# Norms of two key blocks as four rows: one root and one reciprocal for a pair, spread to the lanes by small products

## The chip, the cores and the metric

The kernel runs on one core of a Trainium2 chip. The metric is the time of one execution on the device, in microseconds (us), the median of several runs. TensorE (PE in the profile, its weight loads PEld) multiplies and writes to PSUM, VectorE (DVE) and ScalarE (ACT) work on SBUF and PSUM, GpSimd (POOL) on SBUF, SyncE (SP) issues most transfers. Each engine takes its instructions strictly in the order in which they stand in its queue.

## The reference, cut to what matters

The kernel computes two layers of a diffusion backbone on 128 context and 2048 latent positions (2176 in all) with 1024 channels. The change concerns the second layer, RWKV-7 time mixing, and there the keys:

```
xr, xw, xk, xv, xa, xg = [u + dx * rw['mu'][i] for i in range(N_LERP)]
k = xk @ rw['w_rkvz'][1]
kk = heads(kf * rw['k_k'].astype(f32))                       # 16 heads of 64 channels
kk = kk * lax.rsqrt(jnp.sum(kk * kk, axis=-1, keepdims=True) + 1e-12)
```

So each head's 64 channels of `kk`, at each position, are divided by the length of that vector of 64.

## The kernel before, in words

The projections of layer 1 (`phase_l1_proj`) hold channels on the partitions (lanes) and positions on the free axis. Three passes follow each other: pass 0 makes r and the decay's hidden layer, pass 1 (`wi == 1`) makes k, its normalised form kk and the hidden layer of a, the third makes v. Passes 0 and 1 go over five segments of positions (450, three times 448, and 384 columns). In each segment DVE and ACT blend the inputs (`lerp`, lines 818 and 819, after the sums of line 803), GpSimd subtracts the rounded part (line 34), and PE makes eight blocks of 128 channels (two heads each) with 24 matmuls a block (lines 832 to 835) and one more block for the hidden layer (`pl`).

For each of the eight k blocks DVE copies the product from PSUM to a tile `o` (line 867), ACT squares it into `sq` (line 871), and `normalise` follows one block later: PE multiplies `sq` with `bones`, a 128x128 matrix of two blocks of ones, so that every lane holds its head's sum (line 846, full fp32, in the trace as two matmul records); ACT takes the root (847), DVE the reciprocal (848), and one DVE operation multiplies `o`, the weight and the reciprocal (849). SP writes the result to `kkC` (line 840).

Rings of buffers tie these steps: four `sq`, five `o`, four PSUM banks for `p`, one PSUM bank for `pnt`. A new `sq` waits for the write of the block four earlier, a new `o` for the last reader of the tile five earlier.

The order on each engine is set by a scheduler when the program is built, from its own cost estimates. It is fixed in the program and shown below where it matters.

Of the kernel before, what the change touches and what calls it, by code (L numbers as in the profile page):

```python
# [7 lines left out]
F32 = mybir.dt.float32  # L8
F32R = mybir.dt.float32r
AF = mybir.ActivationFunctionType  # L10
ALU = mybir.AluOpType
# [4 lines left out]
P = 128  # L16
# [618 lines left out]
def ucol(t):  # L635
    return 1 if t == 0 else 3 + t * P
# [89 lines left out]
def phase_l1_proj(tc, g, ins):  # L726

    nc = tc.nc
# [8 lines left out]
    with ExitStack() as es:  # L737
# [33 lines left out]
        pl = es.enter_context(tc.tile_pool(name="ppl", bufs=2, space=PSUM, reuse_waits="tile"))  # L771
        pn = es.enter_context(tc.tile_pool(name="ppn", bufs=1, space=PSUM, reuse_waits="tile"))
        mu1, muh, kkw, bones, eps = g.l1

        def pieces(c0, n):

            if c0 == 1:
                return [(0, 0, LP), (LP + 2, LP, n - LP - 2)]
            return [(0, c0 - 3, n)]

        def wsplit(parts, src, ncols, ring):
            wh, wl = parts
            for c in range(0, ncols, P):
                w = next(ring)
                nc.sync.dma_start(out=w, in_=src[:, c:c + P].rearrange("(k p) c -> p k c", p=P))
                split_hi(nc, wh[:, :, c:c + P], w)
                split_lo(nc, wl[:, :, c:c + P], w, wh[:, :, c:c + P])
            return wh, wl
# [49 lines left out]
        def chunked(dst, b, o, pcs):  # L838
            for (o0, t0, ln) in pcs:
                nc.sync.dma_start(out=dst[t0 // 64:(t0 + ln) // 64, :, b, :].rearrange("c p t -> p c t"),  # L840
                                  in_=o[:, o0:o0 + ln].rearrange("p (c t) -> p c t", t=64))

        def normalise(b, o, sq, n, pcs):

            pnt = pn.tile([P, 512], F32, name="pnt")
            nc.tensor.matmul(pnt[:, :n], bones, sq[:, :n], start=True, stop=True)
            nc.scalar.activation(sq[:, :n], pnt[:, :n], AF.Sqrt, bias=eps)
            nc.vector.reciprocal(sq[:, :n], sq[:, :n])
            nc.vector.scalar_tensor_tensor(sq[:, :n], o[:, :n], kkw[:, b:b + 1], sq[:, :n], op0=ALU.mult, op1=ALU.mult)
            chunked(g.kkC, b, sq, pcs)  # L850


        for wi, (mi, si, sw, dst) in enumerate(((0, 1, "w1", g.rC), (2, 4, "a1", g.kC))):
            W = [wsplit((W0, W1)[hh], ins["w_rkvz"][wi][:, hh * 512:(hh + 1) * 512], 512, early if (wi, hh) == (0, 0) else w_ring)
                 for hh in range(2)]
            Sw = wsplit(Ws, ins[sw], P, w_ring)
            for (c0, n) in FSEG:
                pcs = pieces(c0, n)
                us = load_u(c0, n)
                ss = sums(us, n)  # L860
                xh, xl = lerp(us, ss, mi, n, 0)
                yh, yl = lerp(us, ss, si, n, 1)
                pend = []
                for b in range(KC):
                    p = fm_block(*W[b // 4], b % 4, xh, xl, n, pd, "p")
                    o = op.tile([P, 512], F32, name="o")
                    nc.vector.tensor_copy(o[:, :n], p[:, :n])
                    chunked(dst, b, o, pcs)
                    if wi == 1:
                        sq = op.tile([P, 512], F32, name="sq", bufs=4)  # L870
                        nc.scalar.activation(sq[:, :n], p[:, :n], AF.Square, scale=kkw[:, b:b + 1])
                        pend.append((b, o, sq))
                    if b == KC - 1:
                        p = fm_block(*Sw, 0, yh, yl, n, pl, "pl")
                        o = op.tile([P, 512], F32, name="o")
                        nc.scalar.activation(o[:, :n], p[:, :n], AF.Tanh if wi == 0 else AF.Copy)
                        for (o0, t0, ln) in pcs:
                            for e in range(2):
                                nc.sync.dma_start(out=g.hwa[e, 64 * wi:64 * wi + 64, t0:t0 + ln], in_=o[64 * e:64 * e + 64, o0:o0 + ln])
                    if len(pend) > 1:  # L880
                        normalise(*pend.pop(0), n, pcs)
                if pend:
                    normalise(*pend.pop(), n, pcs)

        W = [wsplit((W0, W1)[hh], ins["w_rkvz"][2][:, hh * 512:(hh + 1) * 512], 512, w_ring) for hh in range(2)]
        Sw = wsplit(Ws, ins["g1"], P, w_ring)
        for seg in TSEG:
            c0 = ucol(seg[0])
            n = ucol(seg[-1]) + P - c0
# [4 lines left out]
            p = fm_block(*Sw, 0, yh, yl, n, pl, "pl")  # L894
            o = op.tile([P, 512], F32, name="o")
            nc.scalar.activation(o[:, :n], p[:, :n], AF.Sigmoid)
            nc.scalar.dma_start(out=g.sgd[:, c0:c0 + n], in_=o[:, :n])
            for hh in range(2):
                for t in seg:
                    o0 = ucol(t) - c0  # L900
                    p = pd.tile([P, 512], F32, name="p")
# [3 lines left out]
                    o = op.tile([P, 512], F32, name="o")  # L905
# [828 lines left out]
def constants():  # L1734
    import numpy as np

    f32 = np.float32
    d = {"ident": np.eye(P, dtype=f32)}
    n = np.arange(512)
    s = 1.0 / math.sqrt(LS * 128)  # L1740
    ang = lambda k, m: 2 * np.pi * (np.outer(m, k) % LS) / LS
    d["dft"] = (np.stack([np.cos(ang(2 * n, n)), np.cos(ang(2 * n + 1, n)), np.sin(ang(2 * n, n)),
                          np.sin(ang(2 * n + 1, n + 1))]) * s).astype(f32)
    sign = np.where(np.arange(513) % 2 == 0, s, -s)
    row = np.zeros((1, 514))
    row[0, :513] = sign
    d["dft_row"] = row.astype(f32)
    col = np.zeros((P, 2))
    col[:, 0] = sign[:P]
    d["dft_col"] = col.astype(f32)  # L1750
    a = 2 * np.pi * (np.outer(np.arange(P), np.arange(P)) % P) / P
    d["c128"] = np.stack([np.cos(a), np.sin(a), np.cos(a) / P, -np.sin(a) / P], 1).astype(f32)
    m = np.full((9, P, 512), 1e30, f32)
    q = np.arange(P)
    for t, (ra, cb) in enumerate(TYPES):
        (r0, nr), (c0, ncol) = RT[ra], CT[cb]
        r, c = ra * 8 + q // 16, cb * 16 + q % 16
        kr = ra * 8 - 4 + r0 + np.arange(nr)
        kc = cb * 16 - 8 + c0 + np.arange(ncol)
        rs, cs = np.clip(r - 4, 0, 24), np.clip(c - 8, 0, 48)  # L1760
        okr = (kr[None] >= rs[:, None]) & (kr[None] < rs[:, None] + 8)
        okc = (kc[None] >= cs[:, None]) & (kc[None] < cs[:, None] + 16)
        m[t, :, :nr * ncol] = np.where(okr[:, :, None] & okc[:, None, :], 0, 1e30).reshape(P, -1)
    d["namask"] = m
    st, t, up = np.arange(P)[:, None] % 64, np.arange(64)[None], np.arange(P)[:, None] >= 64
    d["tri"] = np.stack([st < t, st <= t, np.where(up, st >= t, st <= 63 - t), np.where(up, st <= 63 - t, st >= t),
                         63 - st < t], 1).astype(f32)
    d["bones"] = np.kron(np.eye(2), np.ones((64, 64))).astype(f32)
    return d


# [61 lines left out]
```

## Time and profile before

| | |
|---|---|
| median of 3 runs | 4006.51 us (3995.91 to 4013.2) |
| the profiled execution | 4006.46 us, span 4004.7 us |
| mean granted TensorE clock | 0.905 of full speed |
| busy share of the span: PE, DVE, ACT, POOL | 88%, 65%, 43%, 20% |
| pass 1 (k), by the first of its matmuls and the first of pass v | 1641 to 1923 us of the span |

Busy shares over the whole span mix stages with different limits; pass 1 is read on its own below. A matmul's duration in the trace holds its way through the array; back-to-back matmuls overlap, so that what one costs is the distance between starts.

### The profile page before, as it was taken

The page shows a single profiled execution, that of the slowest core. Times are in us where ns is not written, and L with a number is a line of the kernel's source. Part 1 is how long each engine was busy: PE and PEld are TensorE (multiplying, and loading weights), DVE is VectorE, ACT ScalarE, POOL GpSimd, SP SyncE. Part 2 cuts the span into 40 slices and gives each one's busy share as a digit, 9 for nine tenths or more (in the row PEclk, how much of TensorE's full clock was granted, in tenths as well). Part 3 has the DMA queues.
Part 4 walks back from the last instruction along what each step waited for, and adds up shares of the span by engine and source line. Part 5 has one row for each costly group of instructions (what it writes and reads, how often), then busy time and mean ns, then how long its engine had stood idle before and what let it go on. Part 6 is the DMA issues. An engine that isn't in the chain of part 4 may idle for free. (4 is left out here: it accounts for less than half of the span.)

```text
span 4004.7 us, 93003 instructions
## 1 busy us (share of the span) xinstructions
PE 3509.4 (88%) x39520; PEld 3039.7 (76%) x39520; DVE 2597.0 (65%) x4364; ACT 1730.1 (43%) x3629; POOL 782.3 (20%) x434
## 2 busy tenths in 40 slices
PE   6999998889999979999899997888888888885677
PEld 3999997567777769888687776877888778884555
DVE  6201101478867765899862347877878878875997
ACT  5110011266645533544442344555565555543444
POOL 3000000332202223323332320000000000001665
PEclk8999998999999989999899997788778888787888
DMA  6122214565546742434315542333233233224543
GB/s 213 64 71 86 69 58 139 159 172 143 135 121 191 186 111 81 135 103 115 119 67 153 157 122 79 88 92 86 78 92 86 78 92 98 76 76 152 202 165 115
DMA packets 514383, 463.07 MB, mean 116 GB/s; under 512 B 217111, under 2 KB 420391, under 8 KB 512430
## 3 DMA queue, kind: packets, MB, share of 16 engines
q1 hardware_dynamic: 506350, 444.95, 38.1%
q10 hardware_dynamic: 7616, 12.16, 0.9%
q8 instruction: 310, 5.08, 0.5%
q14 instruction: 107, 0.88, 0.1%
HBM read 314.13 MB, written 129.48 MB: 111 GB/s over the span
## 5 line engine op out<-in xcount | busy, mean ns | idle before, releaser
L34 POOL TENSOR_TENSOR xl<-xt,xh 128x1792 fp32r<-128x1792 f32 (+4 forms) x64 | 246.8, 3867 | 487.8 <-ACT xh L30 244.3
L40 PE MATMUL p<-ul,wh 128*128 128x436 f32 (+1 forms) x800 | 291.7, 365 | 2.4 <-DVE ul L34 2.1
L38 PE MATMUL p<-uh,wh 128*128 128x436 f32 (+1 forms) x800 | 291.5, 365 | 0.0
L39 PE MATMUL p<-uh,wl 128*128 128x436 f32 (+1 forms) x800 | 289.7, 362 | 0.0
L819 DVE SCALAR_TENSOR_TENSOR xt<-s,l1s,xt 128x448 f32<-128x448 f32 (+4 forms) x256 | 246.8, 1016 | 46.7 <-ACT xt L818 46.7
L834 PE MATMUL p<-xh,w 128*128 128x448 f32 (+2 forms) x640 | 240.4, 376 | 17.7 <-ACT w L30 10.2
L1213 POOL COPY WC<-W 128x8 f32<-128x8 f32 x68 | 29.8, 438 | 1133.4 <-DVE Sc L1455 671.4
L835 PE MATMUL p<-xh,w 128*128 128x448 f32 (+2 forms) x640 | 239.7, 374 | 0.0
L30 ACT ACTIVATE xh<-xt 128x1792 fp32r<-128x1792 f32 (+4 forms) x64 | 99.8, 1570 | 226.7 <-DVE xt L819 107.0
L1265 PE MATMUL pq<-Xb,BKb 64*128 64x64 f32 x2176 | 162.5, 304 | 37.6 <-DVE OM L1276 28.2
L1340 DVE TENSOR_TENSOR xe<-xe,l1s 128x31 f32<-128x31 f32 (+15 forms) x527 | 180.8, 343 | 18.1
L1339 DVE TENSOR_TENSOR l1s<-xe,xe 128x31 f32<-128x31 f32 (+15 forms) x527 | 179.6, 341 | 16.4
L1265 PEld LDWEIGHTS pq<-Xb,BKb 64*128 64x128 f32 x2176 | 151.2, 215 | 46.8 <-DVE OM L1276 31.0
L818 ACT ACTIVATE xt<-u,l1s 128x448 f32<-128x448 f32 (+4 forms) x256 | 142.0, 625 | 61.5 <-POOL xl L34 46.0
L40 PEld LDWEIGHTS p<-ul,wh 128*128 128x128 f32 x800 | 151.8, 190 | 12.6 <-DVE ul L34 4.5
L38 PEld LDWEIGHTS p<-uh,wh 128*128 128x128 f32 x800 | 151.9, 190 | 7.8 <-ACT uh L30 0.3
L39 PEld LDWEIGHTS p<-uh,wl 128*128 128x128 f32 x800 | 152.1, 190 | 7.5
L34 DVE TENSOR_TENSOR wl<-w,wh 128x2048 fp32r<-128x2048 f32 x12 | 27.5, 2291 | 189.5 <-ACT wh L30 189.5
L832 PE MATMUL p<-xl,w 128*128 128x448 f32 (+2 forms) x640 | 148.4, 369 | 1.1 <-POOL xl L34 1.1
L434 POOL TENSOR_TENSOR kl<-ld,kh 128x1088 fp32r<-128x1088 f32 x16 | 42.2, 2659 | 547.8 <-ACT kh L433 547.5
L834 PEld LDWEIGHTS p<-xh,w 128*128 128x128 f32 x640 | 123.6, 193 | 32.5 <-ACT w L30 11.1
L1303 PE MATMUL pq<-ident,BKb 64*128 64x64 f32 x1088 | 62.0, 256 | 92.0 <-DVE OM L1276 44.8
(375 smaller groups left out, 10036.9 us busy)
## 6 DMA issues: line engine op xcount, KB each, us to landing
x<-x SPq DMA_DIRECT2D x34, 512.0 KB
zu<-u1T SPq DMA_DIRECT2D x34, 512.0 KB
kk<-kkC SPq DMA_DIRECT2D x68, 256.0 KB
k<-kC SPq DMA_DIRECT2D x68, 256.0 KB
r<-rC SPq DMA_DIRECT2D x68, 256.0 KB
sv<-v SPq DMA_DIRECT2D x136, 128.0 KB
x<-in_x_sample SPq DMA_DIRECT2D x32, 512.0 KB
wmod<-in_ada_w SPq DMA_DIRECT2D x16, 1024.0 KB
```

The costliest lines, as they stand in the source:

```text
L34: (eng or nc.vector).tensor_tensor(lo, x, hi.bitcast(F32), op=ALU.subtract)
L38: nc.tensor.matmul(out, ah, bh, start=start, stop=False)
L39: nc.tensor.matmul(out, al, bh, start=False, stop=False)
L40: nc.tensor.matmul(out, ah, bl, start=False, stop=stop)
L818: nc.scalar.activation(x[:, j], us[hh][:, j, 1:n + 1], AF.Copy, scale=mu1[:, i, k:k + 1])
L819: nc.vector.scalar_tensor_tensor(x[:, j], ss[hh][:, j, :n], muh[:, i, k:k + 1], x[:, j], op0=ALU.mult, op1=ALU.add)
L832: nc.tensor.matmul(p[:, :n], w(wh, k), xl[:, k, :n], start=False, stop=(k == KC - 1))
L834: nc.tensor.matmul(p[:, :n], w(wh, k), xh[:, k, :n], start=(k == 0), stop=False)
L835: nc.tensor.matmul(p[:, :n], w(wl, k), xh[:, k, :n], start=False, stop=False)
L1265: nc.tensor.matmul(o[:, h, p], BK[HF[h], p, 64 * h:64 * h + 128], X[HF[h], p, 0:64], start=True, stop=True)
L1339: nc.vector.tensor_tensor(t, L[:, m:, j:m].to_broadcast([P, n, m]), Tm[:, j:m, :m].to_broadcast([P, n, m]), op=ALU.mult)
L1340: nc.vector.tensor_tensor(o, o, t, op=ALU.subtract)
```

## The change

The matrix `bones` is replaced by columns: for block i of a pair, four columns that pick the two heads of that block into rows 2i and 2i+1. `normalise` now takes two blocks at a time, once three are pending. Two products (line 848 of the changed kernel) accumulate the four head sums in lanes 0 to 3; ACT takes the root and DVE the reciprocal on these four rows. For each block, second first, two products with four rows and 64 columns of a repeated column of the identity (line 856) write each head's reciprocal to its 64 lanes in PSUM, and the DVE multiplication (858) reads it there. Lines of the changed kernel stand 1 to 9 higher from here on: 867 is 876, 871 is 880, 819 is 820, 832 to 835 are 833 to 836, 847 is 850, 848 is 851.

```diff
+        heads = bones[:, 0:8].rearrange("p (i h) -> p i h", i=2)
...
-        def normalise(b, o, sq, n, pcs):
+        def normalise(pend, n, pcs):

             pnt = pn.tile([P, 512], F32, name="pnt")
-            nc.tensor.matmul(pnt[:, :n], bones, sq[:, :n], start=True, stop=True)
-            nc.scalar.activation(sq[:, :n], pnt[:, :n], AF.Sqrt, bias=eps)
-            nc.vector.reciprocal(sq[:, :n], sq[:, :n])
-            nc.vector.scalar_tensor_tensor(sq[:, :n], o[:, :n], kkw[:, b:b + 1], sq[:, :n], op0=ALU.mult, op1=ALU.mult)
-            chunked(g.kkC, b, sq, pcs)
+            for i, (b, o, sq) in enumerate(pend):
+                nc.tensor.matmul(pnt[0:4, :n], heads[:, i], sq[:, :n], start=(i == 0), stop=(i == 1))
+            inv = pend[0][2][0:4]
+            nc.scalar.activation(inv[:, :n], pnt[0:4, :n], AF.Sqrt, bias=eps[0:4])
+            nc.vector.reciprocal(inv[:, :n], inv[:, :n])
+            for i in (1, 0):
+                b, o, sq = pend[i]
+                pnt = pn.tile([P, 512], F32, name="pnt")
+                for h in range(2):
+                    nc.tensor.matmul(pnt[64 * h:64 * h + 64, :n], g.ident[0:4, 2 * i + h:2 * i + h + 1].to_broadcast([4, 64]), inv[:, :n],
+                                     start=True, stop=True)
+                nc.vector.scalar_tensor_tensor(sq[:, :n], o[:, :n], kkw[:, b:b + 1], pnt[:, :n], op0=ALU.mult, op1=ALU.mult)
+                chunked(g.kkC, b, sq, pcs)
...
-                    if len(pend) > 1:
-                        normalise(*pend.pop(0), n, pcs)
+                    if len(pend) > 2:
+                        normalise([pend.pop(0), pend.pop(0)], n, pcs)
                 if pend:
-                    normalise(*pend.pop(), n, pcs)
+                    normalise(pend, n, pcs)
...
-    d["bones"] = np.kron(np.eye(2), np.ones((64, 64))).astype(f32)
+    pair = np.kron(np.eye(2), np.ones((64, 1)))
+    d["bones"] = np.concatenate([pair, 0 * pair, 0 * pair, pair, np.zeros((P, P - 8))], 1).astype(f32)
```

On PE, inside a block of a 448 column segment, before (`xh`, `xl` are the rounded input and its rest, `w` a weight half, `pnt` the norm's bank, `l1s` the tile that holds `bones`; a row of L846 is one product):

```order
L835 MATMUL p<-xh_12258,w_12226 128x448
L834 MATMUL p<-xh_12258,w_12225 128x448
L846 MATMUL pnt<-sq,l1s 128x448 [waits Activation_49]
L835 MATMUL p<-xh_12258,w_12226 128x448
L834 MATMUL p<-xh_12258,w_12225 128x448
L835 MATMUL p<-xh_12258,w_12226 128x448
L832 MATMUL p<-xl_12259,w_12225 128x448 x8
```

On PE in a 448 column segment of the changed kernel, at the end of a block:

```order
L835 MATMUL p<-xh_12258,w_12220 128x448
L856 MATMUL pnt<-sq,ident 64x448 [waits DVE_49]
L856 MATMUL pnt<-sq,ident 64x448
L836 MATMUL p<-xh_12258,w_12221 128x448
L833 MATMUL p<-xl_12259,w_12220 128x448 x8
L856 MATMUL pnt<-sq,ident 64x448 [waits DVE_49]
L856 MATMUL pnt<-sq,ident 64x448
L848 MATMUL pnt<-sq,l1s 4x448 [waits DVE_49]
L848 MATMUL pnt<-sq,l1s 4x448
L835 MATMUL p<-xh_12258,w_12220 128x448 [waits Activation_49]
```

Where one product per block stood among the matmuls, waiting for ACT's square alone, a pair now has three places on PE, each waiting for DVE: twice for the spreading products, once for the sums, which here stand right behind the spreading products of the pair before, and use the same bank. Over the whole pass the sums follow the last spreading products of the pair before with no matmul between in 9 of 19 places; the two spreading groups of a pair stand side by side in 2 of 20; and 28 to 52 matmuls stand between the sums and the first spreading.

On DVE at the start of the pass, before (`sq` the squares, later the result; `o` the copied product):

```order
L848 RECIPROCAL sq<-sq 128x450 [waits Activation_49]
L867 COPY o<-p 128x450 [waits DMAHW2_49,DMAHW1_49,PE_49]
L849 SCALAR_TENSOR_TENSOR sq<-o,l1s,sq 128x450 [waits DVE_49]
L848 RECIPROCAL sq<-sq 128x450 [waits Activation_49]
L867 COPY o<-p 128x450 [waits DMAHW6_49,DMAHW5_49,PE_49]
L849 SCALAR_TENSOR_TENSOR sq<-o,l1s,sq 128x450 [waits DVE_49]
```

On DVE in the changed kernel, a little later in the pass:

```order
L851 RECIPROCAL sq<-sq 4x450 [waits Activation_49]
L858 SCALAR_TENSOR_TENSOR sq<-o,l1s,pnt 128x450 [waits DMAHW6_49,DMAHW5_49,PE_49]
L876 COPY o<-p 128x448 [waits DMAHW3_49,DVE_49]
L858 SCALAR_TENSOR_TENSOR sq<-o,l1s,pnt 128x450 [waits PE_49]
L876 COPY o<-p 128x448 [waits DVE_49]
L851 RECIPROCAL sq<-sq 4x448 [waits DMAHW5_49,DMAHW4_49,Activation_49]
```

One reciprocal serves two blocks; each multiplication now waits for PE, and the copies behind it wait for a multiplication, whose `o` they take over.

## Rows read from the trace of the kernel before

**Rows 1.** The page's busy times of the whole execution.
```profile
span 4004.7 us, 93003 instructions
PE 3509.4 (88%) x39520; PEld 3039.7 (76%) x39520; DVE 2597.0 (65%) x4364; ACT 1730.1 (43%) x3629; POOL 782.3 (20%) x434
```

**Rows 2.** Busy time of each engine in stretches of the span: pass 1 from 1660 to 1960 us, then a stretch of pass v.
```profile
core 0: us, PE busy (x) PEld busy (x) DVE busy (x) ACT busy (x) POOL busy (x), PEclk, DMA share, GB/s
...
1660.00:1720.00 60.00, 53.51 (x237) 45.66 (x237) 56.29 (x45) 30.28 (x43) 21.20 (x5) 0.94 0.41 113
1720.00:1780.00 60.00, 55.12 (x241) 46.76 (x242) 58.28 (x47) 29.93 (x45) 18.13 (x5) 0.96 0.38 100
1780.00:1840.00 60.00, 58.55 (x267) 50.79 (x267) 59.55 (x50) 25.75 (x39) 17.34 (x4) 0.99 0.36 98
1840.00:1900.00 60.00, 55.65 (x270) 49.97 (x269) 57.33 (x52) 28.21 (x43) 13.91 (x4) 0.97 0.45 123
1900.00:1960.00 60.00, 48.27 (x201) 38.66 (x200) 58.00 (x46) 29.55 (x40) 21.76 (x6) 0.86 0.40 110
...
2000.00:2050.00 50.00, 50.00 (x226) 41.55 (x225) 29.59 (x31) 17.65 (x23) 16.95 (x5) 1.00 0.26 92
```

**Rows 3.** What PE waited for between 1640 and 1950 us: total us, times, longest.
```profile
PE pnt L846 <- ACT sq L871: 21.2, 8, 5.9
PE p L38 <- ACT xh L30: 3.8, 1, 3.8
PE pnt L846 <- ACT sq L847: 2.4, 1, 2.4
PE pl L835 <- DVE ws L34: 1.1, 1, 1.1
PE p L832 <- POOL xl L34: 1.1, 2, 0.6
PE p L834 <- ACT xh L30: 0.8, 1, 0.8
PE p L39 <- POOL xl L34: 0.6, 1, 0.6
```

**Rows 4.** Groups of DVE's instructions from 1640 to 1965 us by shape: count, busy us, mean ns of one, idle time before them.
```profile
L848 DVE RECIPROCAL sq<-sq 128x448 f32<-128x448 f32 x24 | 70.6, 2940 | 4.3 <-ACT sq L847 4.3
...
L819 DVE SCALAR_TENSOR_TENSOR xt<-s,l1s,xt 128x448 f32<-128x448 f32 x48 | 46.9, 1025 | 0.7 <-ACT xt L818 0.7
...
L848 DVE RECIPROCAL sq<-sq 128x450 f32<-128x450 f32 x8 | 23.7, 2961 | 3.5 <-ACT sq L847 3.5
...
L848 DVE RECIPROCAL sq<-sq 128x384 f32<-128x384 f32 x8 | 20.2, 2529 | 0.0
...
L803 DVE TENSOR_TENSOR s<-u 128x1792 f32<-128x1792 f32 x6 | 19.4, 3235 | 0.0
L849 DVE SCALAR_TENSOR_TENSOR sq<-o,l1s,sq 128x448 f32<-128x448 f32 x24 | 19.1, 797 | 0.1
```

**Rows 5.** One norm product among PE's matmuls, in order of time: start, us, instruction (x2: its two records).
```profile
1731.96 0.37 PE L835 MATMUL p<-xh,w 128*128 128x448 f32 x1
1732.17 0.91 PE L846 MATMUL pnt<-sq,l1s 128*128 128x448 f32 x2
1732.57 0.71 PE L834 MATMUL p<-xh,w 128*128 128x448 f32 x1
...
1733.12 0.37 PE L835 MATMUL p<-xh,w 128*128 128x448 f32 x1
1733.33 0.37 PE L834 MATMUL p<-xh,w 128*128 128x448 f32 x1
```

**Rows 6.** Fp32 products on narrow parts of the array in an earlier stage, in order of time. L107 puts sixteen records of 256 columns on four column strips of 32 in turn; L122 has two columns of weights; L461 and L462 use the whole array.
```profile
1121.28 1.07 PE L107 MATMUL pm<-wmod,sc 128*32 128x256 f32 x16
1122.28 0.39 PE L461 MATMUL s<-ch,qs 128*128 128x256 f32 x1
...
1123.90 0.34 PE L461 MATMUL s<-kh,qs 128*128 128x384 f32 x1
1124.07 0.34 PE L462 MATMUL s<-kl,qs 128*128 128x384 f32 x1
1124.35 0.59 PE L122 MATMUL pm<-m,sel 128*2 128x256 f32 x2
1124.87 0.31 PE L497 MATMUL pt<-ident,pr 128*96 128x128 f32 x1
```

**Rows 7.** What ACT's squares waited for between 1640 and 1965 us: total us, times, longest.
```profile
ACT sq L871 <- DMA kkC<-sq: 34.1, 10, 6.1
ACT sq L871 <- DVE o L867: 32.7, 12, 5.2
```

**Rows 8.** A DVE operation of the same kind with one input in PSUM, in a later stage (512 columns).
```profile
L947 DVE SCALAR_TENSOR_TENSOR zo<-zo,pg 128x512 f32<-128x512 f32 x34 | 23.4, 687 | 3.8 <-DVE zo L946 0.5
```

**Rows 9.** The norm's products and roots, all of the execution: count, shortest, median and longest ns, first and last start, shapes.
```profile
L846 PE MATMUL pnt<-sq,l1s x80: 484/539/1121, 1665.4 to 1936.4; 128*128 128x448 f32 x48, 128*128 128x450 f32 x16, 128*128 128x384 f32 x16
L847 ACT ACTIVATE sq<-pnt,eps x40: 557/627/637, 1673.1 to 1938.7; 128x448 f32<-128x448 f32 x24, 128x450 f32<-128x450 f32 x8, 128x384 f32<-128x384 f32 x8
```

## The prediction

> **What bounds the kernel now.** PE is busy for 88% of the span and DVE for 65% [rows 1], but the change touches only pass 1, so I read that pass by itself, first in the busy times by stretch. From 1660 to 1960 us DVE is busy for 56.29 + 58.28 + 59.55 + 57.33 + 58.00 = 289 of 300 us, PE for 271 [rows 2]. DVE is full here. PE is busy for all 50 of 50 us in the pass that follows, where DVE has 20 us in 50 to spare [rows 2], so what pass 1 gains or loses should go on to the end.
>
> A full DVE would make this a clear gain if PE merely waited for it. So the second view is PE's waits. They come to 21.2 + 3.8 + 2.4 + 1.1 + 1.1 + 0.8 + 0.6 = 31 us [rows 3]. Of these 24 us stand before the norm products, and 21 of those wait for ACT's squares. The squares in turn wait for DVE's copies (32.7 us) and for the write that frees their buffer (34.1 us) [rows 7]: DVE is late, its copies are late, the squares are late. That is all that a lighter DVE can give back: at most 31 us. Outside these waits PE has matmuls to do, and DVE's 97% and PE's own work are nearly level. The question is then what the change puts on PE.
>
> **The change part by part.**
>
> DVE and ACT. 20 of 40 reciprocals go. They cost 70.6 + 23.7 + 20.2 = 114.5 us [rows 4], and as the duration follows the columns and not the rows (2940 ns at 448, 2529 at 384), a reciprocal of 4 rows should take what one of 128 takes: 57 us less on DVE, 289 to 232. 20 of 40 roots of 0.627 us go too [rows 9], 12.5 us of ACT. Neither is worth this in time: it is worth the waits that it removes, 0 to 31 us. The multiplication now reads one operand from PSUM. The nearest row has 687 ns for 512 columns [rows 8], against a mean of 797 ns now at 448 with both operands in SBUF [rows 4]: nothing, or 0.1 to 0.2 us each to the good on an engine that will no longer be full. I take zero. The constants are as large as before, and kkC has as many writes; the second block of a pair is written first.
>
> PE, the sums. The duration of a record holds its way through the array, so I take the price from starts. From 1731.96 to 1733.33 us stand three ordinary matmuls and one norm product [rows 5]: 1.37 us, and the ordinary ones start 0.205 us apart (1733.12, 1733.33), so the product costs 1.37 - 3 x 0.205 = 0.755 us. With 4 columns of weights instead of 128 it should cost the same: L122, with two columns, still takes 0.52 us from start to start for 256 columns [rows 6], and 0.755 x 256/448 is 0.43. 40 products before, 40 sums after: nothing.
>
> PE, the spreading. 80 new fp32 products, two for each block. The two of a block write different halves of the lanes. On neighbouring strips such products run at once: the sixteen records of L107 would take 16 x 0.216 = 3.45 us in a row (half of the 0.43 for each record), and the next matmul starts 1.00 us after the first [rows 6]. So I price two halves as one product. At a mean of 436 columns (8 of 450, 24 of 448, 8 of 384 by [rows 9]) one is 0.734 us, times 40 blocks: 29 us.
>
> The Trainium skill has a rule that speaks against it: the page "TensorE: Matmul & The Clock Gate", in Part 3 under what overlaps, says that a weight load overlaps a running matmul only where the row groups differ, and the two halves here use the same four rows. By that rule much of the second half would come after the first. The trace of L107 contradicts it, since its strips share all 128 rows; so the sum stays with 29 us, and the rule stands below as a rival.
>
> PE, the changes of shape. L122 starts 0.28 us after an L462 of 384 columns, which on the pitch of L461 before it (0.17 us) should have been 0.17; and it holds the next instruction for 0.52 instead of 0.43 us [rows 6]. Going to a narrow shape and back thus costs about 0.11 + 0.09 = 0.2 us. Behind L107 it is 1.00 - 0.86 = 0.14 us. By the order, each pair has three such trips (sums, two spreadings), 60 in all; 9 sums stand right behind a spreading and save half a trip, 2 spreadings side by side save one. That is 53 to 54 trips at 0.2: 10 us, or 0 if these small gaps are something else, or 15 if a strip of 4 rows drains worse. The page "TensorEngine Tiling (Array Packing)", under Key Properties, says that changing the tiling mode drains TensorE; it gives no time for it, and these rows agree that there is one.
>
> PE, the waits. Old: 31 us. New ones are sure. Where a sum stands directly behind a spreading (9 places), or two spreadings side by side (2), the second must wait until DVE's multiplication has freed the one bank: the matmul's way out (0.37 - 0.205 = 0.17 us) and the multiplication (0.69 by [rows 8]), 0.86 us: 11 x 0.86 = 9 us. Between the sums and the first spreading stand 28 to 52 matmuls of 0.205, 5.7 to 10.7 us, against 0.17 + 0.63 + 2.94 = 3.7 us for way, root and reciprocal: covered, unless DVE has other work in front. It has: each segment has 16 blends of 1.025 us and two sums of 3.235 [rows 4], 23 us in bursts of four and more (4.1 us, 7.3 with a sum), and a multiplication or reciprocal behind one makes PE wait, since PE's queue now contains that wait itself. Before, a late DVE cost PE 8 waits of 2.65 us on average through the squares [rows 3]. I take as many again, 21 us. So 9 + 21 = 30 us of new waits against 31 of old: zero, with both ends kept, all waits gone (-31) and the new on top of some of the old (+20).
>
> The sum: 29 + 10 + 0 = 39, about 40 us on a bound of 4006.5 us. The profiled execution (4006.46) is the median to within 0.1 us, so no correction: **4046 us**, 1.0% slower. About 0.5% (20 us) is what a measurement of this kernel can tell from no change.
>
> **The rivals.**
>
> *The lighter DVE pays for it (not slower).* With DVE at 232 of 300 us the squares come in time and the bursts leave room, so PE's 31 us of waits go. For it: 24 of them trace back to DVE. Against: 11 places with a wait that the order makes certain. Then 4006.5 + 39 - 31 = 4015, and 4005 if the shape changes are free too. This decides only if less than some 10 us of waits are left in the pass. Faster by 0.5% needs the spreading itself hidden, which PE's full queue does not allow.
>
> *The chain of a pair becomes the bound.* Sums (1.5 + 0.1 + 0.17), root 0.63, reciprocal 2.94, spreading with its way out 1.03, multiplication 0.69, and the last two again: 8.8 us in series, on one PSUM bank. If a quarter of a segment's 23 us of blends (5.7) falls inside, a pair takes 14.5 us. PE's own work for a pair is 216 x 0.205 / 4 + 4 x 0.755 + 0.6 = 14.7. They are level, so any lateness of 0.8 to 1.7 us a pair adds 16 to 34 us: 4062 to 4080. For it: `o`, `sq` and the bank are held longer than before, and the squares already wait for buffers [rows 7].
>
> *The halves run one after the other*, by the rule above: 29 us more, 4075. Against it stands L107; for it, that no row here has two tiles of 4 rows and 64 columns.
>
> **How the numbers follow.** My forecast, 4028 to 4062: 0.60. The chain: 0.13. The halves in series: 0.08. The lighter DVE, 4003 to 4026: 0.17. Faster by more than 20 us: 0.02. The range runs from within the lighter-DVE case to the top of the chain's, **4012 to 4078**. Slower by over 0.5%: 0.60 + 0.13 + 0.08 = 0.81, less a little for the low edge, 0.79; same 0.19; faster 0.02.
>
> **What would show it.** In pass 1 after: 20 reciprocals of 2.5 to 2.96 us; DVE busy nearer 230 than 289 us in 300 and waiting for PE before the multiplication; the two products of a block starting together and taking one product's time; PE's waits moved from the squares to DVE's multiplications and reciprocals, near 30 us in all; the first matmul of pass v about 40 us later. I am wrong if PE's waits shrink below 10 us, if the halves start 0.7 us apart, or if the waits at the two new places exceed 50 us.

## The result, and the profile after

The changed kernel takes 4062.9 us (median of 4 runs, 4056.8 to 4070.0) against 4004.8 us for the kernel before: a ratio of 1.0146, 95% interval 1.0117 to 1.0175, or 58 us (47 to 70) slower. The forecast was 4046 us in a range of 4012 to 4078 and slower, with 0.79: sign and range hold. The size does not quite: 58 us in place of 40, just past the upper edge of what I called my forecast (4028 to 4062), where the rival of the chain began. Why is the question of the experiments.

The page of the changed kernel, against [rows 1]: PE has 51 us more of busy time, DVE 64 us less.

```profile
span 4064.6 us, 93282 instructions
...
PE 3560.3 (88%) x39680; PEld 3040.3 (75%) x39680; DVE 2532.7 (62%) x4344; ACT 1724.8 (42%) x3611; POOL 782.9 (19%) x434
```

Busy times of the changed kernel by stretch of pass 1, which answer to [rows 2]; the first matmul of pass v starts at 1987 us here.

```profile
core 0: us, PE busy (x) PEld busy (x) DVE busy (x) ACT busy (x) POOL busy (x), PEclk, DMA share, GB/s
1660.00:1720.00 60.00, 53.24 (x231) 40.07 (x232) 42.65 (x37) 28.12 (x38) 19.82 (x5) 0.94 0.38 106
1720.00:1780.00 60.00, 56.03 (x232) 40.29 (x231) 30.40 (x30) 15.62 (x22) 9.44 (x4) 0.91 0.25 66
1780.00:1840.00 60.00, 52.06 (x220) 35.33 (x218) 34.64 (x33) 18.15 (x25) 12.54 (x3) 0.94 0.28 73
1840.00:1900.00 60.00, 56.17 (x246) 41.86 (x247) 38.14 (x34) 20.50 (x31) 14.01 (x4) 0.97 0.31 82
1900.00:1960.00 60.00, 43.38 (x183) 32.00 (x182) 45.09 (x46) 28.92 (x42) 27.30 (x6) 0.83 0.50 137
```

From 1660 to 1960 us DVE is busy for 191 us, not 289. It is full in none of these rows. PE is idle for 39 of these 300 us, and its granted clock is 0.83 to 0.97.

What PE waited for in the changed kernel between 1640 and 2010 us (total us, times, longest), against [rows 3]. L848 is a sum, L856 a spreading product, L858 the multiplication, L851 the reciprocal, L880 the square, L835 and L836 the projection.

```profile
PE pnt L848 <- DVE sq L858: 13.5, 12, 3.0
PE pl L835 <- ACT xh L30: 10.4, 3, 6.2
PE pnt L848 <- ACT sq L880: 5.8, 1, 5.8
PE pnt L856 <- DVE sq L858: 5.4, 4, 2.1
PE pnt L856 <- DVE sq L851: 2.7, 2, 2.4
PE p L835 <- ACT sq L880: 2.6, 1, 2.6
PE pl L833 <- POOL xl L34: 2.3, 1, 2.3
PE pl L836 <- DVE ws L34: 2.1, 1, 2.1
PE p L833 <- POOL xl L34: 1.1, 2, 0.6
PE p L835 <- ACT xh L30: 0.7, 1, 0.7
```

They come to 46.6 us where [rows 3] has 31. The squares, 21.2 us before, are down to 5.8 us, one wait at the start of the pass that the kernel before has too (5.8 of its 21.2), and 2.6 us for a PSUM bank of the projection that a square reads last. In their place stand 13.5 + 5.4 = 18.9 us before products that want the one bank back from the multiplication, and 10.4 us for the high parts that ACT makes.

DVE's groups against [rows 4, 8], then what DVE and ACT waited for (ACT against [rows 7]), all of the changed kernel between 1640 and 2010 us:

```profile
L851 DVE RECIPROCAL sq<-sq 4x448 f32<-4x448 f32 x12 | 35.3, 2938 | 19.8 <-ACT sq L850 18.0 <-DMA kkC<-sq 1.8
...
L858 DVE SCALAR_TENSOR_TENSOR sq<-o,l1s,pnt 128x448 f32<-128x448 f32 x24 | 16.2, 675 | 48.3 <-PE pnt L856 48.3
```
```profile
DVE sq L858 <- PE pnt L856: 65.9, 22, 6.3
DVE sq L851 <- ACT sq L850: 29.7, 10, 7.6
...
ACT sq L880 <- DMA kkC<-sq: 104.9, 21, 12.7
```

A reciprocal of 4 rows takes 2938 ns where one of 128 took 2940, and the multiplication takes 675 ns with an operand in PSUM. DVE now waits for PE. ACT waits three times as long (104.9 against 34.1 us) for a squares buffer to be written out; by the code a buffer is now held until its pair is done.

### The profile page after: what moved, and what is told of

Read it like the earlier page. It is cut to its first block, busy times and chain, and to the rows that moved or that the text cites. A ratio compares the mean times of both kernels' runs of the same rounds, so it can differ in the third digit from the quotient of the medians.

```text
span 4064.6 us, 93282 instructions
## 1 busy us (share of the span) xinstructions
PE 3560.3 (88%) x39680; PEld 3040.3 (75%) x39680; DVE 2532.7 (62%) x4344; ACT 1724.8 (42%) x3611; POOL 782.9 (19%) x434
## 5 line engine op out<-in xcount | busy, mean ns | idle before, releaser
L820 DVE SCALAR_TENSOR_TENSOR xt<-s,l1s,xt 128x448 f32<-128x448 f32 (+4 forms) x256 | 262.5, 1078 | 51.7 <-ACT xt L819 51.6
L38 PE MATMUL p<-uh,wh 128*128 128x436 f32 (+1 forms) x800 | 291.3, 364 | 0.0
L835 PE MATMUL p<-xh,w 128*128 128x448 f32 (+2 forms) x640 | 239.7, 375 | 20.1 <-ACT w L30 10.2
L836 PE MATMUL p<-xh,w 128*128 128x448 f32 (+2 forms) x640 | 237.1, 370 | 0.0
L835 PEld LDWEIGHTS p<-xh,w 128*128 128x128 f32 x640 | 124.7, 195 | 45.3 <-ACT w L30 11.1
L38 PEld LDWEIGHTS p<-uh,wh 128*128 128x128 f32 x800 | 151.8, 190 | 7.8 <-ACT uh L30 0.3
```

The lines of the kernel that those rows point to most:

```text
L38: nc.tensor.matmul(out, ah, bh, start=start, stop=False)
L820: nc.vector.scalar_tensor_tensor(x[:, j], ss[hh][:, j, :n], muh[:, i, k:k + 1], x[:, j], op0=ALU.mult, op1=ALU.add)
L835: nc.tensor.matmul(p[:, :n], w(wh, k), xh[:, k, :n], start=(k == 0), stop=False)
L836: nc.tensor.matmul(p[:, :n], w(wl, k), xh[:, k, :n], start=False, stop=False)
```

## The measure used below, and the table

A run's time scatters by 10 us and more, mostly in the stages after pass v: from the last product of pass v to the end the profiled executions below take 1850 to 1878 us, and no edit touches that part. The kernel before ran in every series, with medians of 4005 to 4013 us, and each ratio is taken to the runs of its own series. Each profile also gives a second number, the stretch from the first projection matmul of pass 1 to the last L38 of pass v. The lines that give its end, for the kernel before and for the changed one (durations in ns, then first and last start in us):

```profile
L38 PE MATMUL p<-w,xh x272: 389/396/792, 1923.2 to 2148.0; 128*128 128x512 f32 x136
```
```profile
L38 PE MATMUL p<-w,xh x272: 388/394/502, 1987.0 to 2212.8; 128*128 128x512 f32 x136
```

and its start, from the time lines of the two:

```profile
1641.05 0.47 PE L834 MATMUL p<-xh,w 128*128 128x450 f32 x1 [0.83 <-ACT xh L30]
```
```profile
1640.50 0.47 PE L835 MATMUL p<-xh,w 128*128 128x450 f32 x1 [0.66 <-ACT xh L30]
```

That is 506.9 us before and 572.3 after, 65 us more. "Time" is the ratio's distance from 1, times 4006 us; its 95% half-width is 5 to 8 us, 9 to 12 for the changed kernel and the copy by ACT. Each stretch is of one execution, by the same two rows of each profile; first starts lie between 1635 and 1645 us. How far the stretch scatters was not measured. Its part from the first to the last L38 is the same work in all kernels but for a few of pass 1's last products, and takes 212 to 228 us (272 with the roots on GpSimd); so differences of some 10 us or less in the stretch are not told from scatter.

| kernel | banks | ratio | time, us | stretch, us |
|---|---|---|---|---|
| before | 1 | 1 | 0 | 0 |
| before | 2 | 0.9965 | -14 | -1 |
| half the reciprocals left out | 1 | 1.0019 | +8 | -2 |
| half the reciprocals left out | 2 | 0.9950 | -20 | -11 |
| spreading's products added | 1 | 1.0050 | +20 | +23 |
| both of these | 2 | 1.0039 | +16 | +27 |
| changed | 1 | 1.0146 | +58 | +65 |
| changed, ACT empties the bank | 1 | 1.0153 | +61 | +72 |
| changed, whole weights | 1 | 1.0121 | +48 | +43 |
| changed | 2 | 1.0057 | +23 | +30 |
| changed, reciprocals apart | 2 | 1.0075 | +30 | +34 |
| changed, whole weights | 2 | 1.0047 | +19 | +25 |
| the same with fp32r products | 2 | 1.0028 | +11 | +10 |
| before, half the roots on GpSimd | 2 | 1.3003 | +1203 | +1208 |

## The experiments

**A second bank for the changed kernel.**

```
-        pn = es.enter_context(tc.tile_pool(name="ppn", bufs=1, space=PSUM, reuse_waits="tile"))
+        pn = es.enter_context(tc.tile_pool(name="ppn", bufs=2, space=PSUM, reuse_waits="tile"))
```

> The changed kernel with two PSUM banks for the sums and the spreading products in place of one; nothing else differs. In the trace of the changed kernel PE waits 46.6 us between 1640 and 2010 us, and 13.5 + 5.4 = 18.9 us of it stand before a sum or a spreading product and end with the multiplication that frees the one bank. If PE's own added work is most of the loss (trips to the narrow shapes at about 1.09 us for a block, some 46 us in all), the second bank gives back 10 to 19 us: 40 to 50 us over the kernel before, a ratio of 1.010 to 1.0125, and the waits of L848 for L858 are gone. If the chain of a pair on its one bank is the bound, nearly all of the loss goes: below 20 us over the kernel before, under 1.005. If the waits only move to the next cause (squares, lerps), the time stays near 58 us over, 1.0146.

1.0057 (1.0043 to 1.0071): 36 us come back, twice what the waits named for the bank had been; 23 us over the kernel before lies between my first expectation (40 to 50) and my second (below 20). PE's waits now begin so:

```profile
PE pnt L848 <- DVE sq L858: 8.6, 5, 3.2
PE p L835 <- ACT sq L880: 6.2, 3, 3.5
PE pnt L848 <- ACT sq L880: 5.8, 1, 5.8
```

The waits for the bank fall from 18.9 to 8.6 us, and the 10.4 us for the high parts of the hidden layer are gone with them; how the one brings the other was not followed. The edit also changed the order that was built for PE: by the time lines the two spreadings of a pair now stand side by side in all 20 pairs (2 with one bank), and no sum stands directly behind a spreading (9 with one bank). Busy times over the whole stretch, the changed kernel with one bank, then with two:

```profile
1640.50:2212.80 572.30, 526.26 (x2278) 399.92 (x2279) 354.34 (x338) 216.86 (x304) 170.66 (x45) 0.95 0.33 95
```
```profile
1640.81:2177.70 536.89, 509.21 (x2278) 394.38 (x2279) 356.69 (x338) 216.16 (x304) 171.76 (x45) 0.98 0.35 101
```

PE is idle for 18 us less (46.0, 27.7) and busy for 17 us less with as many records, at a granted clock of 0.98 in place of 0.95. A small part of the 17 is the order: two spreadings side by side share one way in and out, 0.3 us a pair, and the 9 sums share none any more; some 4 us in all, an estimate from the trips priced below. The rest, some 13 us, goes with the clock. One place shows it. The time line of PE with one bank, and the busy times of the last stretch in it:

```profile
1750.06 0.97 PE L856 MATMUL pnt<-sq,ident 4*64 4x450 f32 x4
1751.82 0.97 PE L856 MATMUL pnt<-sq,ident 4*64 4x450 f32 x4 [0.79 <-DVE sq L858]
1753.57 3.00 PE L848 MATMUL pnt<-sq,l1s 128*4 128x448 f32 x4 [0.79 <-DVE sq L858]
1756.51 0.74 PE L835 MATMUL p<-xh,w 128*128 128x448 f32 x1
```
```profile
1754.00:1757.00 3.00, 3.00 (x5) 0.75 (x4) 0.18 (x1) 0.96 (x2) 0.00 (x0) 0.50 0.86 215
```

and such places with two banks:

```profile
1749.31 1.72 PE L856 MATMUL pnt<-sq,ident 4*64 4x448 f32 x8
1750.96 0.47 PE L835 MATMUL p<-xh,w 128*128 128x448 f32 x1
...
1755.04 1.67 PE L848 MATMUL pnt<-sq,l1s 128*4 128x448 f32 x4
1756.64 0.47 PE L833 MATMUL p<-xl,w 128*128 128x448 f32 x1
```

The two spreadings and the sums of the next pair take 6.45 us from first start to the next projection matmul; with two banks 1.65 and 1.60, 3.25 us. Two waits of 0.79 us explain half of that. Behind them the granted clock is 0.50, the 1.2 GHz level, and the sums take 3.00 us in place of 1.67. Each of these two waits, which I had priced at 0.86 us, comes to 1.6 us here.

**The second bank without the change**, the same edit in the kernel before.

> The kernel before with two PSUM banks for the norm products in place of one; nothing else differs. It tells what the second bank is worth without the change. PE waited there 2.4 us, once, for the root that frees the bank [rows 3]. If the bank matters only where the multiplication holds it, the time stays: 0.998 to 1.001. If a second bank is worth 10 us or more by itself, 0.9975 or less, then a part of the 36 us that it gave the changed kernel is no cost of the change.

0.9965 (0.9951 to 0.9979), 14 us faster: the best kernel of all here that computes everything, faster than the kernel before and the changed one. But the stretch is only 1 us shorter, and PE's waits for the root are as they were (2.5 us in four places for 2.4 in one). The gain is not seen in the pass in which the bank is used; what makes it is open, and some may be scatter (the kernel before had a median of 4013 us in this series, the highest of all). The two measures part here. By the time, and by my own second expectation, 14 of the 36 us that the second bank gave the changed kernel are no cost of the change; by the stretch 1 of 35. So between 22 and 35 us are the change's.

**A lighter DVE alone.**

```
+            if b % 2:
+                nc.vector.scalar_tensor_tensor(sq[:, :n], o[:, :n], eps, pnt[:, :n], op0=ALU.mult, op1=ALU.mult)
+            else:
                 nc.scalar.activation(sq[:, :n], pnt[:, :n], AF.Sqrt, bias=eps)
                 nc.vector.reciprocal(sq[:, :n], sq[:, :n])
...
```

> The kernel before with the root and the reciprocal of every second block left out: that block is multiplied by a constant and by the sums straight from PSUM, so half the norms are not computed. DVE has the changed kernel's load (20 reciprocals less, 57 us) and PE the kernel before's. It measures what the lighter DVE alone is worth. My theory: at most the 31 us that PE waited in pass 1, likely 10 to 31 us faster, 0.992 to 0.9975, with PE's waits before the norm products mostly gone. If a lighter DVE is worth nothing, because PE is the bound: 1.000. If DVE, at 97% busy, was the true bound: 31 us or more faster, below 0.992.

1.0019 (1.0006 to 1.0032): nothing gained, which looks like the second expectation, PE being the bound. PE's waits give another reason:

```profile
PE pnt L846 <- DVE sq L848: 17.9, 4, 4.9
PE pnt L846 <- ACT sq L874: 5.8, 1, 5.8
```

The waits for squares (21.2 us, [rows 3]) fell to 5.8, as the theory wants. But L848, DVE's multiplication, now reads the bank, and DVE comes to it late: up to 4.9 us. The run tells of relief and of the bank at once, so it was made again with two banks.

> The kernel before with the root and the reciprocal of every second block left out, as in the run with one bank (half the norms are not computed), and two PSUM banks. With one bank the lighter DVE brought nothing (1.0019), and PE waited 17.9 us, four times up to 4.9 us, for the multiplication that now frees the bank. If that hold is why, the second bank lets the relief through: PE's waits in the pass fall below 15 us and the time is 8 to 25 us shorter than with one bank, 0.996 to 1.000. If a lighter DVE is worth nothing anyway, because PE's own work is the bound, the time stays at 1.001 to 1.003.

0.9950 (0.9938 to 0.9962), 28 us less than with one bank, of which the second bank gave the kernel before 14 as well. Beside the kernel before with two banks, the lighter DVE alone is worth 6 us of time, which the two intervals do not tell from nothing, and 10 us of the stretch: at most a third of the 31 us that I gave as its most. PE still waits 24.6 us, 14.9 of them for squares, where I expected below 15 in all.

**PE's new products alone**, into a bank that nobody reads.

```
             nc.tensor.matmul(pnt[:, :n], bones, sq[:, :n], start=True, stop=True)
+            for h in range(2):
+                nc.tensor.matmul(extra[64 * h:64 * h + 64, :n], g.ident[0:4, h:h + 1].to_broadcast([4, 64]), sq[0:4, :n], start=True, stop=True)
```

> The kernel before with the two half products of the spreading added behind each block's norm product, into a spare PSUM bank that nobody reads; their operand is four rows of the squares. PE has the changed kernel's new products and no new wait, DVE and ACT have the load of before. It measures what PE's work alone costs. My theory: 40 trips of about 1.09 us, 43 us, less what goes of the 31 us of waits, since a later PE leaves DVE more time: 15 to 43 us slower, 1.004 to 1.011. If the full DVE hides PE's work: under 10 us, 1.0025 or less. If the work alone explains the whole loss: 55 us or more, 1.0137.

1.0050 (1.0035 to 1.0065), 20 us. Busy times over the whole stretch, here and in the kernel before:

```profile
1637.22:2167.00 529.78, 512.40 (x2278) 403.60 (x2279) 417.59 (x358) 225.20 (x322) 165.91 (x45) 0.97 0.36 102
```
```profile
1641.05:2148.00 506.95, 474.15 (x2118) 399.97 (x2119) 412.45 (x358) 222.05 (x321) 165.05 (x44) 0.96 0.37 106
```

PE is busy for 38 us more with 160 more records, where 40 trips of 1.09 us would be some 43 (its granted clock is 0.97 for 0.96), and idle for 15 us less (32.8, 17.4): the work fills waits that DVE's lateness had made. Under a full DVE about half of it is hidden.

**Both, without the pair**: the relief, two banks, and the added products in the bank that the norm product overwrites.

> The kernel before with two banks, with the root and the reciprocal of every second block left out (half the norms are not computed), and with two half products ahead of each block's norm product, into the bank that the norm product then overwrites. DVE has the relief and PE the spreading's work of the changed kernel, but there is no pair: no row of four that all wait for, and no buffer held for a partner. Without the added products this kernel is 20 us faster than the one before; the changed kernel with two banks is 21.5 us slower. If PE's own work is what lies between them, 40 trips of 1.09 us put it at 15 to 25 us slower, 1.004 to 1.0065. If the work takes the place of waits, as where it was added to the kernel before (43 us of work for 19 us of time), it is at 0.998 to 1.001, and the other 20 us of the changed kernel are the pair's: its chain and the buffers held for it.

1.0039 (1.0023 to 1.0056). Against the same kernel without the products that is 36 us of time and 38 of the stretch for 43 us of work: with DVE relieved, PE's work counts nearly in full. The changed kernel with two banks is 7 us above it in time (3 in the stretch), within the scatter of both measures, so for the pair itself, its chain and its held buffers, no cost is seen once the bank is doubled.

**Whole weights**: both kinds of products on the whole array, by weights filled up with zeros.

```
-                nc.tensor.matmul(pnt[0:4, :n], heads[:, i], sq[:, :n], start=(i == 0), stop=(i == 1))
+                nc.tensor.matmul(pnt[:, :n], hw[:, i], sq[:, :n], start=(i == 0), stop=(i == 1))
...
-                for h in range(2):
-                    nc.tensor.matmul(pnt[64 * h:64 * h + 64, :n], g.ident[0:4, 2 * i + h:2 * i + h + 1].to_broadcast([4, 64]), inv[:, :n],
-                                     start=True, stop=True)
+                nc.tensor.matmul(pnt[:, :n], sel[:, 128 * i:128 * i + 128], pend[0][2][:, :n], start=True, stop=True)
```

> The changed kernel with the same sums and the same spreading, but with weights filled up with zeros to 128 x 128, so that each sum and each spreading is one product on the whole array (one spreading product for a block in place of two halves): no change of shape anywhere, the same bank, the same order. By my working a whole product of 448 columns costs 0.755 us; the trace of the changed kernel shows about 1.09 us for a block's two halves with their way in and out, and 0.28 us more for a pair's sums than twice 0.755. So 40 x 0.35 + 20 x 0.28 = 20 us should go: about 39 us over the kernel before, 1.008 to 1.011. If the changes of shape cost nothing and the 58 us are waits, nothing goes: 1.0145. If the two halves in truth ran one after the other, 29 us or more would go: 1.007 or below.

1.0121 (1.0103 to 1.0138), 10 us less than the changed kernel (its own interval is as wide as that), half of the 20 that I had expected; the stretch is 23 us shorter, at a granted clock of 0.97 for 0.95, so part of that is the clock. With two banks:

> The changed kernel with both edits at once: weights filled up with zeros to 128 x 128, so that no product changes the shape, and two PSUM banks. With two banks alone PE is busy for 292.4 us from 1640 us to the first matmul of pass v, with whole weights alone for 283.6 us: the narrow shapes cost some 9 to 14 us of PE's own work. If that is what the whole weights save, and the second bank has already taken the waits, the time is 21.5 - 9 to 14 = 8 to 13 us over the kernel before, 1.002 to 1.0033. If the shapes only cost time because of the one bank (a longer hold), nothing more goes: 1.0057. If the spreading's own 29 us are hidden as well now: 1.000 or less.

1.0047 (1.0034 to 1.0060): 4 us of time and 5 of the stretch below narrow weights with two banks, so the time is not told apart from no gain, and my 8 to 13 us over the kernel before was missed. With two banks the two spreadings of a pair stand side by side (1.72 us for both, above) and share a trip. PE is busy for 9 us less in the stretch (500.2 for 509.2), of which 5 come through. So the changes of shape cost 10 us of time or less.

**Reciprocals in a tile of their own, first block first**, on two banks.

```
-            inv = pend[0][2][0:4]
+            inv = op.tile([P, 450], F32, name="inv", bufs=1)[0:4]
...
-            for i in (1, 0):
+            for i in (0, 1):
```

> The changed kernel with two PSUM banks, with the four reciprocals in a tile of their own, and with the first block of a pair spread and multiplied first, so that the buffer of the squares that ACT wants next is written out first. With two banks ACT still waits 70.8 us, 19 times, for the write of a squares buffer, and PE 12.0 us for squares behind it. If the late buffers cost PE these waits, 5 to 12 us go: 1.003 to 1.0045, and ACT's waits for the write fall by a third or more. If they are slack of ACT, the time stays: 1.005 to 1.0065.

1.0075 (1.0060 to 1.0090), no gain, and ACT's waits for the write are 73.4 us for 70.8. Long as they are, they are slack of ACT, or the order of a pair's two writes does not decide them.

**ACT empties the bank**, on one bank.

```
+                nc.scalar.activation(sq[:, :n], pnt[:, :n], AF.Copy)
-                nc.vector.scalar_tensor_tensor(sq[:, :n], o[:, :n], kkw[:, b:b + 1], pnt[:, :n], op0=ALU.mult, op1=ALU.mult)
+                nc.vector.scalar_tensor_tensor(sq[:, :n], o[:, :n], kkw[:, b:b + 1], sq[:, :n], op0=ALU.mult, op1=ALU.mult)
```

> The changed kernel with its one bank, in which ACT copies each spread block out of PSUM into the squares' buffer and DVE multiplies from there, so that ACT, and not DVE, frees the bank; the 40 copies add some 25 us to ACT, which is busy for 133 of 347 us in the pass. The second bank gave the changed kernel 36 us, and the kernel before 14. If the changed kernel loses the difference because the bank waits for DVE, which has blends and sums in front of the multiplication, ACT's copy gives back 10 to 25 us: 1.008 to 1.012. If it loses it because a bank is used three times in a chain, whoever empties it, the time stays at 1.013 to 1.016 or, with a further step in the chain, goes above. ACT's own late squares would show as longer waits of PE before the copies or the sums.

1.0153 (1.0131 to 1.0176): no gain. PE's waits:

```profile
PE p L835 <- ACT sq L881: 13.4, 5, 5.5
PE pl L835 <- ACT xh L30: 13.3, 3, 6.7
PE pnt L848 <- ACT sq L858: 5.9, 9, 0.7
...
PE pnt L856 <- ACT sq L858: 2.6, 3, 1.3
```

The bank is free earlier (8.5 us of waits for 18.9), but PE's waits for ACT's squares and high parts grow by more. The loss moved to another queue. Whether DVE's other work or the three uses of one bank are to blame, this run does not tell.

**Products of one pass**, on whole weights and two banks: squares, weights and reciprocals as fp32r.

```
...
-                        sq = op.tile([P, 512], F32, name="sq", bufs=4)
+                        sq = op.tile([P, 512], F32R, name="sq", bufs=4)
...
```

> The changed kernel with whole weights and two PSUM banks, and with squares and reciprocals rounded to fp32r, so that each sum and spreading is a product of one pass; the root stays in PSUM, and the product is written in place of the block. (The rounding changes the squares and reciprocals in their low bits.) An fp32 product of 448 columns costs 0.755 us, an fp32r one 0.205 us. 40 sums and 40 spreadings at 0.53 us less (436 columns) are 43 us of PE's work less than with fp32 products: if PE's own work is the bound, 8 to 13 us over the kernel before become 30 to 35 under it, 0.991 to 0.993. If waits for squares, copies and blends take their place, half of it or more is lost: 0.996 to 1.000.

1.0028 (1.0012 to 1.0044), outside both of my expectations (0.991 to 0.993, 0.996 to 1.000). By my prices PE has 43 us less work. Its busy time in the stretch falls by 32 us (467.9 for 500.2, at a granted clock of 0.94 for 0.98), and 8 us come through (15 in the stretch). PE's waits begin so:

```profile
PE p L840 <- ACT sq L884: 22.4, 8, 6.5
PE pnt L853 <- DVE o L862: 8.1, 5, 2.8
```

PE overtakes the squares and waits for the projection's own PSUM banks, which the squares read last. (Writing the product over the block holds that buffer longer, so part of it is this kernel's.) PE's work is not the only bound.

**Half of the roots on GpSimd**, to relieve DVE without PE, on two banks.

```
+            if b % 2:
+                nc.scalar.activation(sq[:, :n], pnt[:, :n], AF.Identity, bias=eps)
+                nc.gpsimd.tensor_tensor(sq[:, :n], sq[:, :n], g.mhalf[:, 0:1].to_broadcast([P, n]), op=ALU.pow)
...
```

> The kernel before with two banks and with the reciprocal root of every second block taken on GpSimd, as the power -0.5 of the sums that ACT brings out of PSUM; all norms are computed. DVE has 20 reciprocals less and PE nothing more. A power of one column takes 0.56 us in an early stage, a subtraction of 1792 columns 4.2 us, so one of 448 columns should take 1 us or, if the power is as slow for a column as DVE's reciprocal, 3 to 5 us; GpSimd is busy for 92 of 283 us in the pass. If 20 us come from the lighter DVE, as where the work was left out, the time is 0.995 to 0.998. If the power is so slow that GpSimd's low parts come late (8 us or more each), it is above 1.003.

1.3003, 1.2 ms slower. GpSimd's groups, first line:

```profile
L849 POOL TENSOR_TENSOR sq<-sq,mhalf 128x448 f32<-128x448 f32 x12 | 861.5, 71804 | 0.0
```

A power of 448 columns takes 72 us, 160 ns a column. The row with one column (0.56 us) had hidden this; my 1 to 5 us were wrong by more than ten times.

## Why the prediction was right in sign and short in size

**DVE and ACT: right.** The reciprocals keep their price with 4 rows (2938 ns), the multiplication is no dearer (675 ns), and the relief was worth nothing by itself, only waits: 10 us of the stretch at most, within my 0 to 31. The waits before the norm's products for squares fell from 21.2 to 5.8 us.

**PE, the spreading: right.** The four records of a block's two halves take 0.97 us from the first start to the last end, where two products in a row would take twice 0.755 us and the way out; the halves run at once. So the rival by the rule of the Trainium skill ("TensorE: Matmul & The Clock Gate", Part 3, what overlaps) falls: halves on the same four rows did not come one after the other here.

**PE, the changes of shape: near.** A lone spreading on the time line of the changed kernel:

```profile
1763.25 0.37 PE L836 MATMUL p<-xh,w 128*128 128x448 f32 x1
1763.54 0.97 PE L856 MATMUL pnt<-sq,ident 4*64 4x448 f32 x4
1764.44 0.47 PE L835 MATMUL p<-xh,w 128*128 128x448 f32 x1
1764.75 0.36 PE L836 MATMUL p<-xh,w 128*128 128x448 f32 x1
```

From 1763.25 to 1764.75 stand two ordinary matmuls and the spreading: 1.50 - 2 x 0.205 = 1.09 us, where I had 0.755 + 0.2; 40 of them are some 43 us. A pair's sums take 1.60 us and 0.2 on the way in and out, where I had 1.51 and 0.2; against the 1.51 us that two products took before, that is 0.3 us a pair, 6 us. The 11 trips that are shared save some 2. PE's own work is thus some 46 us rather than 39, an estimate from these rows. The Trainium skill ("TensorEngine Tiling (Array Packing)", Key Properties) states that a change of tiling mode drains TensorE. The trace agrees, with about 0.1 us on either side of a product.

**PE, the waits: the step that failed.** I set new waits of 9 + 21 = 30 us against 31 us of old ones that would all go: zero. The trace has 46.6. The new waits were not set too low. Of the 16 waits for the bank ten last 0.72 to 0.79 us, 7.8 us in all, where I had 11 x 0.86. The other six last 1.1 to 3.0 us, 11.1 us in all, because DVE came to the multiplication behind blends, sums or weights; with the 2.7 us for the reciprocal these are 13.8 us, where I had 21. The longest of the six on PE, and what stood on DVE just before its multiplication:

```profile
1935.39 0.91 PE L848 MATMUL pnt<-sq,l1s 128*4 128x448 f32 x1 [3.04 <-DVE sq L858]
```
```profile
1931.58 3.16 DVE L820 SCALAR_TENSOR_TENSOR xt<-s,l1s,xt 128x386 f32<-128x386 f32 x1 [3.45 <-ACT xt L819]
```

What failed is the other side of the balance. The old waits did not all go: 14.6 us for squares, inputs and weights stand beside the new ones, the 5.8 us at the start of the pass among them. And 10.4 us for high parts, which I did not foresee, came on top. The two long ones of these (4.1 and 6.2 us) wait for high parts that stand in ACT's queue behind blends, and these blends had waited 2.0 and 3.3 us for GpSimd's low parts; what made that chain late is open. The later of the two:

```profile
1918.97 2.14 ACT L819 ACTIVATE xt<-u,l1s 128x386 f32<-128x386 f32 x4 [3.31 <-POOL xl L34]
```

I also left out the clock altogether. Over the stretch PE is idle for 13 us more than before (46.0 for 32.8) and busy for 52 us more (526.3 for 474.2); some 46 of these are its own work, and the other 6 are matmuls made longer, at a granted clock of 0.95 for 0.96. So of the 25 us that the stretch is beyond my sum (65 less 40) some 7 are PE's own work, 13 idle time and 6 the clock, by estimates from these rows. In time I was 18 us short. The range held because it reached to the top of the chain's case, not because the sum was near.

**The rivals.** That the lighter DVE pays for it is refuted: it is worth some 10 us at most. The chain on one bank is the rival that came true in part: a second bank takes 35 of the 65 us of the stretch away, or 36 of the 58 us of time, 22 to 35 of them by the change. Yet not as I had told it: I let 5.7 us of blends fall inside every pair, and the trace has ten short waits at a bank that is used three times in a pair, six longer ones behind DVE's other work, and a lower clock. Since the second bank also set the spreadings side by side, the bank and the order of PE's queue are not told apart by these runs. The steps from the kernel before to the changed one, each the difference of two kernels above, so that they come to the whole by construction:

| step | stretch, us | time, us |
|---|---|---|
| second bank, kernel before | -1 | -14 |
| reciprocals halved | -10 | -6 |
| spreading's products | +38 | +36 |
| the pair | +3 | +7 |
| one bank again | +35 | +36 |
| sum | +65 | +59 |

**The price of PE's work** I took in full with waits unchanged. Alone it cost 20 to 23 of 43 us under a full DVE and 36 to 38 with DVE relieved: full price and relief belong together, as in the sum. The first matmul of pass v came 63.7 us later (1987.0 for 1923.2), not 40.

Of the signs that I named: halves together, DVE waiting for PE before the multiplication (65.9 us) and 20 reciprocals of the same length came as told; DVE is busy for 191 us in 300, below the 230, since the same work lies in a longer pass; waits "near 30 us in all" did not.

## What to carry to other kernels

When an operation is moved to an engine that is nearly full, price its work there in full, and then look at what it holds: a PSUM bank that the next product needs and another engine empties was a wait in 16 places here, and a second buffer is the first thing to try. An engine at 97% is not by that the bound; relieving DVE was worth 10 us at most where 57 us of its work went, and PE, nearly level with it before, was then busy for 472 of the 496 us of the stretch (two banks). When waits are set against each other, ask of each old one whether it goes, and not only what the new ones cost. Leaving work out, or adding it where nobody reads it, prices a step better than any argument.

## What was not expected of the hardware

- GpSimd's power: 72 us for 128 x 448, against 0.56 us for one column; 61.6 us at 384 columns, so it goes by columns.
- PE's clock: two waits of 0.79 us, with narrow products between, were followed by a granted clock of 0.50 for 3 us, and four records of the sums took 3.00 us in place of 1.67.
- The same addition of 128 x 1792 on DVE takes 3.2 us in the kernel before [rows 4] and 2.0 us in the changed one, while the blends go from 1025 to 1188 ns at 448 columns. No run here tells why.
